# Reading a sub-layer's norm factors from PSUM, adding the last tile's squares inside the product with ones, and keeping the last two row tiles in SBUF

## The chip, the cores and the metric

One core of one Trainium2 chip runs the whole program. The metric is device time in microseconds from the start to the end of one execution. TensorE (PE) multiplies matrices and writes to PSUM; PEld is its weight load. VectorE (DVE), ScalarE (ACT) and GpSimd (POOL) work on elements. SyncE (SP) issues the transfers. Each engine has its own instruction stream and runs it in order.

## The reference, cut to what matters

Two layers. Each has two sub-layers (a mixer and a channel mixer), and the result of each is normalized over the 1024 features, scaled by a gain, and added to the residual `x`. The next sub-layer then normalizes `x` again.

```python
def _rmsnorm(x, w):
    xf = x.astype(jnp.float32)
    y = xf * lax.rsqrt(jnp.mean(xf * xf, axis=-1, keepdims=True) + NORM_EPS)
    return (y * w.astype(jnp.float32)).astype(x.dtype)

for l in range(DEPTH):                     # 2 layers, 512 tokens, 1024 features
    h = _rmsnorm(x, pre_mix_norm[l])
    h = _hybrid_mixer(h, ...)              # ends in  mixed @ w_out
    x = x + _rmsnorm(h, post_mix_norm[l])
    h = _rmsnorm(x, pre_ffn_norm[l])
    h = _conv_glu_ffn(h, ...)              # ends in  (gelu(gate) * val) @ ffn_down
    x = x + _rmsnorm(h, post_ffn_norm[l])
```

## The kernel before, in words

Activations are kept transposed: features on the 128 partitions, the 512 tokens along the free dimension. The residual `x` is eight row tiles of 128x512 (`xs(m)`). Every large product is done with operands split into a high and a low fp32r part, as three matmuls (`mmk`, line 310). Weights stream in as units; ACT rounds one to its high part and DVE or POOL subtracts to get the low part (`wlo`).

The order of instructions on each engine is fixed when the program is built, by a planner (`_Sched`, line 44). Jobs are Python generators; each operation has an estimated cost, each engine an estimated free time, and a job goes on when its planned time has come. Buffers are slots: `get` waits until a slot is planned to be free, `put` gives it back. The chip then runs each engine's stream in that order, held by semaphores.

`out_rows` (line 447) ends a sub-layer and runs four times: mixer and channel mixer of layer 0, then of layer 1. It computes eight result tiles `m` of 128 features.

- The first `full` tiles (five after a mixer, `nt` = 3; seven after a channel mixer, `nt` = 1) are computed for all 512 tokens in one PSUM bank (tag `g`, four banks). `evac` squares the bank into `sq`, adds that to the sum of squares `acc`, and for `m` below 6 writes the bank times the gain to an SBUF tile (tags A, B, C, two each). Tile 6 of a channel mixer stays in its bank.
- The last `nt` tiles, the tail, are computed for tokens 0 to 255 first (half 0) and then for tokens 256 to 511 (half 1). `tail_sum` squares each into the single buffer `vh` and adds it to `acc`. A tail tile below 6 is scaled to SBUF by DVE (`tail_evac`); tiles 6 and 7 stay in their banks.
- For each half, `chain` waits for the tail's sums and calls `row_rstd` (line 356): PE multiplies each 128-token column block of `acc` by a column of ones, which gives sums by token in PSUM; DVE divides by 1024 and adds epsilon; POOL raises to the power -0.5 (tile `rtp`); PE broadcasts the factors to all partitions (tile `pso`, the one bank of tag `o`); ACT copies them to the SBUF tile `rs`.
- Then eight `row` jobs start, 1.1 us apart in the plan. Each multiplies its tile by `rs` (tiles 6 and 7 by gain and `rs`, from PSUM), adds the product to `x` on DVE or POOL, and either stores `x` (end of the program) or has `scale_split` round and split it into `hx`, the input of the next sub-layer.

The next sub-layer begins with `lead`: three output tiles held in three PSUM banks (tag `s`), first over half 0 of `hx`, then over half 1, in the order in which the plan has `hx` ready. Its own factors come from `pre_rstd` (line 624), which uses the same `row_rstd` on the sums of squares `acc2` of the new `x`. The tiles of tags `acc2` and `rs` are free during the tail. While `sc.chain` is set, the low part of a weight unit goes to DVE.

In the profile, tiles are named by tag: A, B, C are the scaled row tiles, `psg`, `pss` and `pso` the PSUM banks, `vh` the tail's squares. All matmuls have line 138, ACT's operations line 147, DVE's and POOL's tensor_tensor line 151, the scalar_tensor_tensor line 165.

Of the kernel before, what the change touches and what calls it, by code (L numbers as in the profile page):

```python
# [10 lines left out]
F32 = mybir.dt.float32  # L11
F32R = mybir.dt.float32r
AF = mybir.ActivationFunctionType
ALU = mybir.AluOpType
# [4 lines left out]
P = 128  # L19
S = 512  # L20
D = 1024
KD = D // P
# [7 lines left out]
EPS = 1e-6  # L30
# [83 lines left out]
def kernel(ctx: ExitStack, tc: tile.TileContext, xT, w_ab, w_cm, w_tm, w_o, w_up, w_dn,  # L114
# [9 lines left out]
    kp = ctx.enter_context(tc.tile_pool(name="kp", bufs=1))  # L124
# [4 lines left out]
    sc = _Sched()  # L129


    def mm(ps, lhsT, rhs, start, stop):
        n = rhs.free_size()
        if rhs.dtype == F32R:
            sc.t += n / 2400.0 if n >= 256 else 0.107
        else:
            sc.t += max(0.214 if lhsT.free_size() > 64 else 0.11, n / 600.0)
        pe.matmul(ps, lhsT, rhs, start=start, stop=stop)  # L138
# [6 lines left out]
    def act(out_, in_, func, after=0.0, **kw):  # L145
        ptr = sum(1 for k in ("scale", "bias") if k in kw and not isinstance(kw[k], float))
        nc.scalar.activation(out_, in_, func, **kw)  # L147
        return sc.op("act", 0.1 + out_.free_size() * 8.3e-4 + 0.09 * ptr, after)

    def tt(out_, a, b, op, after=0.0, eng="dve"):  # L150
        (nc.vector if eng == "dve" else nc.gpsimd).tensor_tensor(out_, a, b, op=op)  # L151
        n = out_.free_size()
        return sc.op(eng, 0.07 + n * 1.05e-3 if eng == "dve" else 0.18 + n * 2.07e-3, after)

    def ts(out_, a, s1, s2, op0, op1=None, after=0.0, eng="dve"):
        e = nc.vector if eng == "dve" else nc.gpsimd
        if op1 is None:
            e.tensor_scalar(out_, a, s1, None, op0=op0)  # L158
        else:
            e.tensor_scalar(out_, a, s1, s2, op0=op0, op1=op1)  # L160
        n = out_.free_size()
        return sc.op(eng, 0.07 + n * 1.0e-3 if eng == "dve" else 0.17 + n * 8.5e-4, after)

    def stt(out_, a, s, b, op0, op1, after=0.0):
        nc.vector.scalar_tensor_tensor(out_, a, s, b, op0=op0, op1=op1)  # L165
        return sc.op("dve", 0.07 + out_.free_size() * 1.05e-3, after)
# [14 lines left out]
    BUFS = {"A": 2, "B": 2, "C": 2, "sq": 2, "acc": 1, "acc2": 1, "vh": 1, "rs": 1}  # L181
    PB = {"g": 4, "s": 3, "o": 1}

    def work(tag, cols=512, dt=F32):
        return kp.tile([P, cols], dt, tag=tag, bufs=BUFS[tag], name=tag)
# [8 lines left out]
    def pget(tag):  # L194
        yield from sc.get("ps" + tag, PB[tag])
        return psum(tag)

    def pput(tag, at):
        sc.put("ps" + tag, at)
# [10 lines left out]
    one = cc[:, C_ONE:C_ONE + 1]  # L210
# [135 lines left out]
    vv = load_vec(0)  # L346
# [6 lines left out]
    rc = load_row(0)  # L353
    sc.set(("vec", 0))

    def row_rstd(acc, seg, dst, tok):

        t0, t1 = seg
        c0, c1 = t0 // P, t1 // P
        ps = yield from pget("o")  # L360
        for c in range(c0, c1):
            mm(ps[:, c:c + 1], acc[:, c * P:(c + 1) * P], one, True, True)
        r = ts(tok[:, c0:c1], ps[:, c0:c1], 1.0 / D, EPS, ALU.mult, ALU.add)
        yield r
        nc.gpsimd.tensor_tensor(tok[:, c0:c1], tok[:, c0:c1], mhalf[:, c0:c1], op=ALU.pow)  # L365
        r = sc.op("pool", 0.17 + 0.15 * (c1 - c0), r)
        yield r
        for c in range(c0, c1):
            mm(ps[:, c * P:(c + 1) * P], tok[:, c:c + 1].to_broadcast([P, P]), ident, True, True)
        r = act(dst[:, t0:t1], ps[:, t0:t1], AF.Copy)  # L370
        pput("o", r)
        return r
# [74 lines left out]
    def out_rows(key, nt, rhs, nk, post, pre, dst, wait_rhs=None, flags=None):  # L447
# [3 lines left out]
        acc = work("acc")  # L451
        hw, sums = {}, []

        full = 8 - nt

        def evac(m, ps):
            if m == 0:
                r = act(acc, ps, AF.Square)
            else:
                sq = yield from wget("sq")  # L460
                r = act(sq, ps, AF.Square)
            if m < 6:
                r2 = ts(hw[m], ps, vv[:, post + m:post + m + 1], None, ALU.mult)
                pput("g", max(r, r2))
            if m:
                yield r
                r = tt(acc, acc, sq, ALU.add, eng="dve" if m == full - 1 else "pool", after=r)
                sc.put("sq", r)
            sc.set((key, "sum", m), r)

        def done(m, ps):
            if m < 6:
                yield from sc.get("ABC"[m % 3], 2)
                hw[m] = work("ABC"[m % 3])
            else:
                hw[m] = ps
            sc.spawn(evac(m, ps), 0)

        m0 = 0
# [53 lines left out]
        for _ in range(nt * ((nk + 7) // 8)):  # L533
            u = yield from take()
            us.append(u)
        yield from sc.get("rs", 1)
        rs = work("rs")
        hx = acc2 = None
        if pre is not None:
            yield from sc.get("acc2", 1)  # L540
            acc2 = work("acc2")
            hx = new_hx()
        left = {"m": 16}

        def row(m, seg, tail, after):
            t0, t1 = seg
            x = xs(m)[:, t0:t1]
            r = rs[:, t0:t1]
            if m < 6:
                h = hw[m][:, t0:t1]  # L550
                d = tt(h, h, r, ALU.mult, after=after)
            else:
                h = (tail[m] if m in tail else hw[m])[:, t0:t1]
                d = stt(h, h, vv[:, post + m:post + m + 1], r, ALU.mult, ALU.mult, after=after)
            yield d
            pool = m in ((1, 3, 5) if pre is not None or not t0 else (0, 1, 3, 4))
            d = tt(x, x, h, ALU.add, after=d, eng="pool" if pool else "dve")
            if m >= 6 and (m in tail or t0):
                pput("g", d)
            if m < 6 and t0:  # L560
                sc.put("ABC"[m % 3], d)
            yield d
            if pre is None:
                sync.dma_start(dst[:, m, t0:t1], x)
            else:
                yield from scale_split(key, m, seg, hx, vv[:, pre + m:pre + m + 1], acc2, d)
            left["m"] -= 1
            left[t0] = left.get(t0, 8) - 1
            if not left[t0]:
                sc.set(("rows", key, t0))  # L570

        def tail_evac(m, ps, seg):
            t0, t1 = seg
# [4 lines left out]
        def tail_sum(m, ps, seg):  # L578
            t0, t1 = seg
            yield sc.t + 0.1  # L580
            sq = yield from wget("vh")
            r = act(sq[:, t0:t1], ps[:, t0:t1], AF.Square)
            yield r
            yield from sc.wait(*[(key, "sum", j) for j in range(full)])
            r = tt(acc[:, t0:t1], acc[:, t0:t1], sq[:, t0:t1], ALU.add, after=r)
            sc.put("vh", r)
            sc.set((key, "tail", m, t0), r)

        def chain(seg, tail):
            t0, t1 = seg  # L590
            yield from sc.wait(*[(key, "tail", m, t0) for m in tail])
            yield sc.t + 0.1
            r = yield from row_rstd(acc, seg, rs, kp.tile([P, 4], F32, tag="rtp", bufs=2, name="rtp"))
            yield r
            for m in range(KD):
                sc.spawn(row(m, seg, tail, r), 0, at=r + 1.1 * m)
            if t0:
                sc.put("acc", r)
                while left["m"]:
                    yield sc.t + 0.2  # L600
                sc.set((key, "out"))

        nu = (nk + 7) // 8
        for seg in HALVES:
            tail = {}
            for i, m in enumerate(range(full, 8)):
                ps = yield from pget("g")
                tail[m] = ps
                for kt in range(nk):
                    mmk(ps, us[i * nu + kt // 8], kt % 8, rhs(kt), seg, kt == 0, kt == nk - 1)  # L610
                    if seg[0] and (kt % 8 == 7 or kt == nk - 1):
                        free(unit=u0 + i * nu + kt // 8)
                    yield
                sc.spawn(tail_sum(m, ps, seg), 0)
                if m < 6:
                    if m not in hw:
                        yield from sc.get("ABC"[m % 3], 2)
                        hw[m] = work("ABC"[m % 3])
                    sc.spawn(tail_evac(m, ps, seg), 0)
            sc.spawn(chain(seg, tail), 0)  # L620
            sc.chain = True
        return hx, acc2, rs

    def pre_rstd(key, acc2, seg, rs, rt):
        yield from sc.wait(*[("sq", key, m, seg[0]) for m in range(KD)])
        r = yield from row_rstd(acc2, seg, rs, rt)
        sc.set(("rs", key, seg[0]), r)
        if seg[1] == S:
            sc.put("acc2", r)
# [931 lines left out]
```

## Time and profile before

| | |
|---|---|
| median of 3 runs | 1411.63 us (1410.67 to 1415.19) |
| profiled execution | 1419.57 us, span 1417.5 us |
| mean granted TensorE clock | 0.981 |
| busy: PE, PEld, DVE, ACT, POOL | 1375.4, 1145.6, 861.9, 618.0, 719.2 us |
| moved by DMA | 123.17 MB |

Times in the trace count from the start of the span. A share of busy time is a mean over stages with different limits, so the stretches around the four calls of `out_rows` are looked at by themselves. A wait is put down to the instruction that came last by the profile.

### The profile page before, as it was taken

To read this page: it belongs to the slowest core of one execution; us is meant where nothing else is said; L and a number is where in the kernel's file an instruction comes from. 1 tells how busy PE (TensorE), PEld (TensorE's weight loads), DVE (VectorE), ACT (ScalarE), POOL (GpSimd) and SP (SyncE) were. 2 spreads that over 40 slices of the span, in tenths; PEclk is the share of its full clock that TensorE was granted. 3 is DMA by queue.
4 is the path that set the end of the run, shared out by engine and by line. 5 is a ranking of instruction groups with operands and counts; after the bars stand their busy time and mean duration, and the time that the engine had idled before them with its cause. 6 is when DMAs were issued, how large, how long until landed. Compare 5 with 4: busy or idle time off the path is not lost. (4 is left out here: it accounts for less than half of the span.)

```text
span 1417.5 us, 19282 instructions
## 1 busy us (share of the span) xinstructions
PE 1375.4 (97%) x7174; PEld 1145.6 (81%) x7174; DVE 861.9 (61%) x1512; ACT 618.0 (44%) x998; POOL 719.2 (51%) x778
## 2 busy tenths in 40 slices
PE   9999999998999999999989999999989999999996
PEld 5878777887888888888878887788888888888886
DVE  4774477847677777421569544778478777773213
ACT  5553466635544344232345433665345444433220
POOL 5455266414577777334173541663155777772441
PEclk9999999999999999999999987999999999999998
DMA  5233111052233232333332330110512333333331
GB/s 200 75 94 87 61 46 45 16 164 75 72 92 104 90 105 89 94 98 99 98 131 68 116 88 16 45 46 23 171 60 79 100 97 98 94 96 88 106 93 60
DMA packets 48701, 123.17 MB, mean 87 GB/s; under 512 B 15584, under 2 KB 18400, under 8 KB 48608
## 3 DMA queue, kind: packets, MB, share of 16 engines
q1 hardware_dynamic: 48608, 121.95, 27.8%
q8 instruction: 57, 0.93, 0.3%
q14 instruction: 36, 0.29, 0.1%
HBM read 115.11 MB, written 6.82 MB: 86 GB/s over the span
## 5 line engine op out<-in xcount | busy, mean ns | idle before, releaser
L151 POOL TENSOR_TENSOR wlo<-raw,whi 128x256 fp32r<-128x256 f32 x560 | 500.8, 925 | 357.9 <-ACT whi L147 343.9
L138 PE MATMUL psg<-hx,whi 128*128 128x512 f32 (+1 forms) x2080 | 631.9, 387 | 2.4 <-DVE hx L151 2.4
L138 PEld LDWEIGHTS psg<-hx,whi 128*128 128x128 f32 x2080 | 379.9, 189 | 76.1 <-DVE hx L151 3.4
L138 PE MATMUL psg<-hx,wlo 128*128 128x512 f32 (+1 forms) x1040 | 396.5, 381 | 0.0
L147 ACT ACTIVATE whi<-raw 128x1024 fp32r<-128x1024 f32 (+1 forms) x200 | 209.0, 1045 | 428.1 <-PE psg L138 367.5
L138 PEld LDWEIGHTS psg<-hx,wlo 128*128 128x128 f32 x1040 | 196.3, 189 | 38.2
L165 DVE SCALAR_TENSOR_TENSOR B<-A,vv,B 128x510 f32<-128x510 f32 (+1 forms) x176 | 199.4, 1135 | 39.3 <-ACT B L147 36.1
L138 PE MATMUL psg<-hid,whi 128*128 128x512 f32 (+1 forms) x744 | 213.1, 371 | 0.0
L138 PEld LDWEIGHTS psg<-hid,whi 128*128 128x128 f32 x744 | 135.6, 188 | 24.1
L151 DVE TENSOR_TENSOR wlo<-raw,whi 128x1024 fp32r<-128x1024 f32 (+1 forms) x58 | 73.7, 1273 | 133.6 <-ACT whi L147 133.6
L138 PE MATMUL psg<-hid,wlo 128*128 128x512 f32 (+1 forms) x372 | 137.9, 371 | 0.0
L138 PE MATMUL psg<-whi,hx 128*128 128x512 f32 x384 | 125.0, 407 | 0.7 <-DVE A L151 0.7
L151 POOL TENSOR_TENSOR acc<-acc,sq 128x256 f32<-128x256 f32 (+1 forms) x65 | 65.8, 1013 | 104.4 <-ACT sq L147 102.5
L151 DVE TENSOR_TENSOR A<-psg,rs 128x512 f32<-128x512 f32 x100 | 68.7, 689 | 40.8 <-PE psg L138 38.8
L138 PEld LDWEIGHTS psg<-whi,hx 128*128 128x128 f32 x384 | 70.1, 191 | 14.6 <-DVE A L151 1.5
L138 PEld LDWEIGHTS psg<-hid,wlo 128*128 128x128 f32 x372 | 70.0, 188 | 12.0
L138 PE MATMUL psg<-wlo,hx 128*128 128x512 f32 x192 | 76.2, 397 | 0.0
L147 ACT ACTIVATE B<-A,vv 128x512 f32<-128x512 f32 x88 | 70.2, 802 | 2.6 <-DVE A L151 2.6
L147 ACT ACTIVATE C<-B 128x512 f32<-128x512 f32 x44 | 27.7, 630 | 86.2 <-DVE B L165 86.1
L151 DVE TENSOR_TENSOR hid<-C,hid 128x512 fp32r<-128x512 f32 x44 | 36.3, 826 | 28.3 <-ACT hid L147 28.3
L158 POOL TENSOR_SCALAR B<-B,den 128x512 f32<-128x512 f32 (+1 forms) x30 | 41.0, 1368 | 23.8 <-DVE den L177 13.7
L138 PE MATMUL pss<-hx,whome 128*128 128x256 f32 x288 | 42.6, 305 | 5.2 <-DVE hx L165 4.6
(239 smaller groups left out, 1704.8 us busy)
## 6 DMA issues: line engine op xcount, KB each, us to landing
raw<-in_w_up_dram SPq DMA_DIRECT2D x88, 512.0 KB, 3.5
raw<-in_w_cm_dram SPq DMA_DIRECT2D x32, 512.0 KB, 3.6
raw<-in_w_dn_dram SPq DMA_DIRECT2D x32, 512.0 KB, 3.5
raw<-in_w_tm_dram SPq DMA_DIRECT2D x24, 512.0 KB, 3.5
raw<-in_w_o_dram SPq DMA_DIRECT2D x16, 512.0 KB, 3.5
raw<-in_w_dn_dram SPq DMA_DIRECT2D x16, 384.0 KB, 3.1
xt<-in_xT_dram SPq DMA_DIRECT2D x7, 512.0 KB, 7.0
scr_a<-am SPq DMA_DIRECT2D x8, 256.0 KB, 2.7
```

Source lines behind the costliest of these rows:

```text
L138: pe.matmul(ps, lhsT, rhs, start=start, stop=stop)
L147: nc.scalar.activation(out_, in_, func, **kw)
L151: (nc.vector if eng == "dve" else nc.gpsimd).tensor_tensor(out_, a, b, op=op)
L158: e.tensor_scalar(out_, a, s1, None, op0=op0)
L165: nc.vector.scalar_tensor_tensor(out_, a, s, b, op0=op0, op1=op1)
```

## The change

`row_rstd` takes a list of sums and sums their products with ones in PSUM. Called by `chain`, it gets the tile `po` of tag `o`, which `out_rows` now takes once and holds for both halves until the last row is done. It leaves the factors there, and `row` multiplies by `po` instead of `rs`. The squares of tile 7 are no longer added to `acc` by DVE: they stay in `vh` and go into the product as a second summand. `vh` is given back when the broadcast has been issued.

Tiles 6 and 7 get SBUF tiles, of the tags `acc2` and `rs`. In `evac` every full tile is scaled to SBUF by DVE; in the tail, ACT writes tiles 6 and 7 times the gain, right behind their Square, and gives the bank back. All rows are then one multiply from SBUF by PSUM and one add. At the end of the program the rows of a half start 0.3 us apart in the plan, and in half 1 POOL adds tiles 0, 2, 4, 6 instead of 0, 1, 3, 4.

```diff
-    def row_rstd(acc, seg, dst, tok):
+    def row_rstd(sums, seg, dst, tok, ps=None):
         t0, t1 = seg
         c0, c1 = t0 // P, t1 // P
-        ps = yield from pget("o")
+        keep = ps is not None
+        if not keep:
+            ps = yield from pget("o")
+        sm = ps[:, t0:t0 + c1 - c0]
         for c in range(c0, c1):
-            mm(ps[:, c:c + 1], acc[:, c * P:(c + 1) * P], one, True, True)
-        r = ts(tok[:, c0:c1], ps[:, c0:c1], 1.0 / D, EPS, ALU.mult, ALU.add)
+            for i, a in enumerate(sums):
+                mm(sm[:, c - c0:c - c0 + 1], a[:, c * P:(c + 1) * P], one, i == 0, i == len(sums) - 1)
+        yield sc.t + 0.1
+        r = ts(tok[:, c0:c1], sm, 1.0 / D, EPS, ALU.mult, ALU.add)
...
             mm(ps[:, c * P:(c + 1) * P], tok[:, c:c + 1].to_broadcast([P, P]), ident, True, True)
+        if keep:
+            return sc.t + 0.1
         r = act(dst[:, t0:t1], ps[:, t0:t1], AF.Copy)
...
-            if m < 6:
-                r2 = ts(hw[m], ps, vv[:, post + m:post + m + 1], None, ALU.mult)
-                pput("g", max(r, r2))
+            r2 = ts(hw[m], ps, vv[:, post + m:post + m + 1], None, ALU.mult)
+            pput("g", max(r, r2))
...
+        def row_tile(m):
+            if m not in hw:
+                tag = "ABC"[m % 3] if m < 6 else ("acc2", "rs")[m - 6]
+                yield from sc.get(tag, BUFS[tag])
+                hw[m] = work(tag)
...
-        yield from sc.get("rs", 1)
-        rs = work("rs")
-        hx = acc2 = None
+        yield from row_tile(6)
+        yield from row_tile(7)
+        acc2, rs = hw[6], hw[7]
+        hx = None
         if pre is not None:
-            yield from sc.get("acc2", 1)
-            acc2 = work("acc2")
             hx = new_hx()
         left = {"m": 16}
+        po = yield from pget("o")
 
         def row(m, seg, tail, after):
             t0, t1 = seg
             x = xs(m)[:, t0:t1]
-            r = rs[:, t0:t1]
-            if m < 6:
-                h = hw[m][:, t0:t1]
-                d = tt(h, h, r, ALU.mult, after=after)
-            else:
-                h = (tail[m] if m in tail else hw[m])[:, t0:t1]
-                d = stt(h, h, vv[:, post + m:post + m + 1], r, ALU.mult, ALU.mult, after=after)
+            r = po[:, t0:t1]
+            h = hw[m][:, t0:t1]
+            d = tt(h, h, r, ALU.mult, after=after)
             yield d
-            pool = m in ((1, 3, 5) if pre is not None or not t0 else (0, 1, 3, 4))
+            pool = m in ((1, 3, 5) if pre is not None or not t0 else (0, 2, 4, 6))
             d = tt(x, x, h, ALU.add, after=d, eng="pool" if pool else "dve")
-            if m >= 6 and (m in tail or t0):
-                pput("g", d)
...
+            if not left["m"]:
+                pput("o", d)
...
             r = act(sq[:, t0:t1], ps[:, t0:t1], AF.Square)
+            if m >= 6:
+                pput("g", act(hw[m][:, t0:t1], ps[:, t0:t1], AF.Copy, scale=vv[:, post + m:post + m + 1]))
+            if m == KD - 1:
+                last[t0] = sq
+                sc.set((key, "tail", m, t0), r)
+                return
             yield r
             yield from sc.wait(*[(key, "sum", j) for j in range(full)])
             r = tt(acc[:, t0:t1], acc[:, t0:t1], sq[:, t0:t1], ALU.add, after=r)
...
             yield from sc.wait(*[(key, "tail", m, t0) for m in tail])
+            yield from sc.wait(*[(key, "sum", j) for j in range(full)])
             yield sc.t + 0.1
-            r = yield from row_rstd(acc, seg, rs, kp.tile([P, 4], F32, tag="rtp", bufs=2, name="rtp"))
+            r = yield from row_rstd([acc, last[t0]], seg, None, kp.tile([P, 4], F32, tag="rtp", bufs=2, name="rtp"),
+                                    po)
+            sc.put("vh", sc.t)
             yield r
+            step = 1.1 if pre is not None else 0.3
             for m in range(KD):
-                sc.spawn(row(m, seg, tail, r), 0, at=r + 1.1 * m)
+                sc.spawn(row(m, seg, tail, r), 0, at=r + step * m)
```

More of the change, by code (lines that the diff above doesn't have):

```diff
@@ L469, in evac @@
             sc.set((key, "sum", m), r)
-        def done(m, ps):
-            if m < 6:
-                yield from sc.get("ABC"[m % 3], 2)
-                hw[m] = work("ABC"[m % 3])
-            else:
-                hw[m] = ps
+        def row_tile(m):
[3 more added lines that the diff above has]
+                hw[m] = work(tag)
+        def done(m, ps):
+            yield from row_tile(m)
             sc.spawn(evac(m, ps), 0)
@@ L547, in row @@
             x = xs(m)[:, t0:t1]
-            r = rs[:, t0:t1]
-            if m < 6:
-                h = hw[m][:, t0:t1]
-                d = tt(h, h, r, ALU.mult, after=after)
-            else:
-                h = (tail[m] if m in tail else hw[m])[:, t0:t1]
-                d = stt(h, h, vv[:, post + m:post + m + 1], r, ALU.mult, ALU.mult, after=after)
+            r = po[:, t0:t1]
+            h = hw[m][:, t0:t1]
+            d = tt(h, h, r, ALU.mult, after=after)
             yield d
-            pool = m in ((1, 3, 5) if pre is not None or not t0 else (0, 1, 3, 4))
+            pool = m in ((1, 3, 5) if pre is not None or not t0 else (0, 2, 4, 6))
             d = tt(x, x, h, ALU.add, after=d, eng="pool" if pool else "dve")
-            if m >= 6 and (m in tail or t0):
-                pput("g", d)
             if m < 6 and t0:
@@ L587, in tail_sum @@
             sc.set((key, "tail", m, t0), r)
+        last = {}
         def chain(seg, tail):
@@ L615, in out_rows @@
                 if m < 6:
-                    if m not in hw:
-                        yield from sc.get("ABC"[m % 3], 2)
-                        hw[m] = work("ABC"[m % 3])
+                    yield from row_tile(m)
                     sc.spawn(tail_evac(m, ps, seg), 0)
@@ L625, in pre_rstd @@
         yield from sc.wait(*[("sq", key, m, seg[0]) for m in range(KD)])
-        r = yield from row_rstd(acc2, seg, rs, rt)
+        r = yield from row_rstd([acc2], seg, rs, rt)
         sc.set(("rs", key, seg[0]), r)
```

## The prediction

> **What bounds the kernel now.** I read the page first, then busy time by stretch, then what TensorE (PE) waited for at each boundary, then the chain at the end.
>
> ```profile
> span 1417.5 us, 19282 instructions
> 320.00:350.00 30.00, 25.03 (x179) 23.18 (x177) 26.70 (x52) 16.80 (x37) 14.80 (x17) 0.94 0.26 85
> 350.00:680.00 330.00, 330.00 (x1475) 273.94 (x1475) 186.75 (x197) 128.24 (x165) 194.83 (x208) 1.00 0.31 94
> 680.00:735.00 55.00, 51.06 (x382) 47.04 (x382) 32.54 (x63) 21.80 (x45) 24.35 (x26) 1.00 0.32 107
> 735.00:1020.00 285.00, 278.29 (x1557) 228.58 (x1557) 184.47 (x447) 141.38 (x257) 123.26 (x136) 0.95 0.23 72
> 1020.00:1066.00 46.00, 41.42 (x287) 38.84 (x286) 31.69 (x61) 21.37 (x46) 19.73 (x24) 0.93 0.23 71
> 1390.00:1418.00 28.00, 15.02 (x124) 14.54 (x122) 12.40 (x29) 1.54 (x4) 6.98 (x9) 0.83 0.23 76
> ```
>
> After each stretch's length come PE, weight loads, VectorE (DVE), ScalarE (ACT), GpSimd (POOL), the granted clock and DMA. In the channel mixer (350 to 680) PE is busy for all 330.00 us: nothing there can be gained by another engine. The changed function runs four times, at the ends of sub-layers. I call these boundaries 1 to 4 (the stretches from 320, 680, 1020 and 1390). PE idles 5.0, 3.9 and 4.6 us in the first three and 13.0 us in the last. DVE is busy 26.7 of 30 us at boundary 1.
>
> What PE waited for around boundaries 1, 2 and 3 (total, times, longest):
>
> ```profile
> PE pso L138 <- DVE acc L151: 2.3, 2, 2.0
> PE pss L138 <- DVE hx L165: 2.0, 4, 0.8
> PE pso L138 <- POOL rtp L365: 0.7, 1, 0.7
> ...
> PE pss L138 <- DVE hx L165: 2.7, 5, 0.8
> ...
> PE pss L138 <- DVE hx L165: 2.6, 2, 2.1
> PE pso L138 <- POOL rtp L365: 1.6, 2, 0.9
> ```
>
> The waits are for the sums (acc), the power (rtp) and the split of the next sub-layer's input (hx), so for the row work that this change touches. The end of the program is a bare chain (start, length):
>
> ```profile
> 1397.44 0.34 PE pso L138 x4
> ...
> 1403.80 0.39 ACT vh L147
> ...
> 1404.22 0.44 DVE acc L151
> ...
> 1404.70 0.62 PE pso L138 x4
> ...
> 1405.58 0.83 POOL rtp L365
> ...
> 1406.45 0.72 PE pso L138 x4
> ...
> 1407.20 0.39 ACT rs L147
> ...
> 1407.62 0.43 DVE A L151
> ...
> 1410.67 0.34 DVE A L151
> ...
> 1414.36 0.42 DVE xt L151
> ```
>
> Square, add, product with ones, power, broadcast, copy, then rows: the last add ends at 1414.78 and the last store follows it by 2.7 us.
>
> **The change, part by part.** Durations first, from the trace by tile (least, median, most, in ns) and the grouped lines (busy us, mean ns):
>
> ```profile
> L151 DVE TENSOR_TENSOR A<-psg,rs x100: 671/692/695, 54.9 to 1282.3; 128x512 f32<-128x512 f32 x100
> L151 DVE TENSOR_TENSOR xt<-xt,psg x16: 405/409/422, 335.9 to 1414.4; 128x256 f32<-128x256 f32 x16
> L151 DVE TENSOR_TENSOR xt<-xt,C 128x256 f32<-128x256 f32 x9 | 6.1, 678 | 0.1
> L151 DVE TENSOR_TENSOR C<-C,rs 128x256 f32<-128x256 f32 x16 | 8.6, 538 | 0.0
> L151 DVE TENSOR_TENSOR B<-B,rs 128x256 f32<-128x256 f32 x16 | 7.8, 486 | 0.0
> L151 DVE TENSOR_TENSOR A<-A,rs 128x256 f32<-128x256 f32 x16 | 7.2, 452 | 4.2 <-ACT rs L147 4.2
> L165 DVE SCALAR_TENSOR_TENSOR psg<-psg,vv,rs 128x256 f32<-128x256 f32 x16 | 7.7, 482 | 0.0
> ```
>
> *Factors stay in PSUM.* One ACT copy (1407.20 to 1407.62, 0.42 us) leaves the chain of each half. The row multiplies now read one operand from PSUM. The rows show what that does: 100 multiplies with a PSUM operand spread over 24 ns while POOL was busy half the time, and the 16 adds that read psg over 17 ns; the same add with both operands in SBUF averages 678 ns. So the multiplies of tiles 0 to 5 fall from 452, 486 and 538 ns to about 411: 0.041 + 0.075 + 0.127 = 0.243, by four of each per boundary, 0.97 us. I take it whole as DVE time.
>
> *Tiles 6 and 7 move to SBUF.* Four multiplies per boundary go from 482 to 411 ns: 0.28 us less. Their four adds lose the PSUM operand: between 0 and 4 x (0.678 - 0.409) = 1.08 us more; I take 0.78, near the upper end, because POOL's work has to overlap something. ACT gets twelve scaled copies of tail tiles for eight factor copies, so four more of 0.39 us in all; its 16.8 of 30 us at boundary 1 cover that, and the copy stands behind the Square on its queue, so the chain does not see it. Uncovered, it would be 0.4 us per boundary. After the channel mixer, tile 6 also costs a full-width DVE scale, while DVE waits for sums: nothing. PSUM banks come free earlier, but no PE wait in the lists is for a bank: nothing.
>
> *The last tile's squares go into the product.* One DVE add per half (1404.22 to 1404.70, 0.48 us) leaves the chain. PE issues four more matmul records per half, 0.34 us by the first row of the chain. Where the squares are late, the first column's sum can be issued ahead, so I charge the exposed chain 0.2. The single vh buffer is now held until half 0's broadcast, so the next half's first Square is later; DVE idles in that stretch, so nothing, else one add's 0.4 us.
>
> *One PSUM tile for both halves.* This adds a wait. The trace shows how two engines share a bank:
>
> ```profile
> DVE A L158 <- ACT acc L147: 27.3, 4, 11.3
> ```
>
> That scale reads a psg bank and waits for the Square that only reads the same bank. If PE and DVE are ordered like that on the new tile, half 1's product must wait for every half 0 multiply placed ahead of it, and the next sub-layer's matmuls queue behind it on PE; multiplies placed behind wait for PE. Before, the products and the fifth and last half 0 multiplies stood so:
>
> ```profile
> 328.66 0.61 PE L138 MATMUL pso<-cc,acc 128*128 128x1 f32 x4 [2.03 <-DVE acc L151]
> 329.99 0.41 DVE L151 TENSOR_TENSOR B<-B,rs 128x256 f32<-128x256 f32 x1
> 334.40 0.48 DVE L165 SCALAR_TENSOR_TENSOR psg<-psg,vv,rs 128x256 f32<-128x256 f32 x1
> 701.37 0.50 PE L138 MATMUL pso<-cc,acc 128*128 128x1 f32 x4
> 701.84 0.41 DVE L151 TENSOR_TENSOR B<-B,rs 128x256 f32<-128x256 f32 x1
> 705.31 0.48 DVE L165 SCALAR_TENSOR_TENSOR psg<-psg,vv,rs 128x256 f32<-128x256 f32 x1
> 1035.36 0.50 PE L138 MATMUL pso<-cc,acc 128*128 128x1 f32 x4
> 1035.73 0.41 DVE L151 TENSOR_TENSOR B<-B,rs 128x256 f32<-128x256 f32 x1
> 1039.67 0.48 DVE L165 SCALAR_TENSOR_TENSOR psg<-psg,vv,rs 128x256 f32<-128x256 f32 x1
> ```
>
> Rows still start 1.1 us apart in the plan at boundaries 1 to 3, so I expect four or five multiplies ahead. Waiting for the fifth would hold the product by 1.74, 0.88 and 0.78 us (330.40 - 328.66 and so on), 3.4 in sum. I take nothing: PE waits for hx afterwards anyway (2.0, 2.7 and 2.6 us), and those waits shrink instead. At boundary 4 the step is 0.3, half 0's rows are done before the product, and nothing waits. The tile is also held until the last row, and the next sub-layer's factors need it; they are computed after the last split already.
>
> The Trainium skill, "PSUM — Partial Sum Buffer", section on bank collisions, speaks here against the change: two engines must not be in one bank at the same time, whatever the columns. The 27.3 us row agrees, for ACT and DVE; by that rule the 3.4 us would be a certain hold of the product and not a possible one.
>
> *Sum for boundaries 1 to 3.* DVE work in the bound stretch falls by 0.97 + 0.28 + 0.48 - 0.78, about 0.95. At boundary 1 DVE limits to the end: -1.0. At boundary 2 two products' 0.34 lie on a busier PE, half of it felt after the waits: -0.5. At boundary 3 what counts is the broadcast of half 1, after which PE runs through: 0.42 + 0.48 less the exposed 0.2, and 0.1 for DVE's lighter load ahead of it: -0.8. Together -2.3; bounds -5.3 (the 7.3 that PE waits for hx there less six extra products of 0.34) and +3.4.
>
> *Boundary 4.* Chain: +0.34 (half 0's products push the last matmul), -0.48 (add), +0.2, -0.42 (copy): -0.36. Then the rows: from 1407.62 to 1414.78 DVE runs 15 instructions in 7.16 us (0.477 each), three of them leftovers of half 0, which now run earlier. Twelve remain: 12 x 0.477 = 5.7 at the old mean, 12 x 0.34 = 4.1 at the undisturbed pitch (the chain's multiply at 1410.67); I take 5.1, as eight are now multiplies with a PSUM operand. That is -2.06; with the chain -2.4, bounds -1.8 and -3.4. POOL still adds four of these rows, others than before, and SyncE's sixteen stores follow the adds in their new order: nothing.
>
> Total: -2.3 - 2.4 = -4.7. The profiled execution took 1419.57 us, 2.07 more than its span, and lies 7.9 us above the median 1411.63; a difference between traces carries over: 1411.63 - 4.7 = **1406.9 us**. Replanning the second mixer (285 us with 6.7 us of PE idle) may add or take 1.5.
>
> **The rivals.**
> - *Only the end gains.* The adds of tiles 6 and 7 collide as often as the multiplies did, and PE's extra products eat the rest. For: adds with two SBUF operands reach 678 ns. Against: boundary 1 is 89% DVE. 1411.63 - 2.4 = 1409.2. The five-multiply hold uncovered gives 1410.3, also no change.
> - *The collisions vanish.* Multiplies immune and nothing shifted to the adds: per boundary 0.97 + 0.28 + 0.48 = 1.73, and 4.1 us at the end: -5.2 - 3.4 = -8.6, 1403.0. For: the 24 ns spread; against: the adds stay exposed. The Trainium skill, "SBUF — State Buffer", section "Who interferes with whom", states it as a rule: a DVE instruction with at most one SBUF input does not contend with GpSimd, one with two does. The rows agree (671 to 695 against 678 for half the elements).
> - *Slower: the bank order.* If all eight half 0 multiplies stand ahead of half 1's product, PE stands until 334.88, 705.79 and 1040.15: 6.2 + 4.4 + 4.8 = 15.4, less the later waits of 2.0 + 2.7 + 2.6: +8.1. With -2.4 that is 1417.3. It decides from the seventh multiply on. Against: the 1.1 us step in the plan.
> - *The end is limited by the stores.* Stores close up as rows do; with 1 us of the gain lost, 1407.9.
>
> **How the numbers follow.** About 0.3% (4.2 us) is what a measurement can tell from no change. Likeliest case 0.40, own range 1404.5 to 1409, two thirds of it beyond 1407.4; collisions vanish 0.15; only the end (with the hold) 0.27; stores 0.06; bank order 0.12. Faster: 0.27 + 0.15 + 0.03; slower 0.12; the rest the same. The range from 1402.5 to 1412.5 leaves out the slower case and a little below.
>
> **What would show it.** No ACT rs copy from rtp factors and no acc add ahead of the last products; multiplies by pso near 411 ns with a narrow spread; adds of tiles 6 and 7 spread like the others; rows of half 0 finished before half 1's product at the end, and the last add 2 to 2.5 us earlier. PE's hx waits at boundaries 1 to 3 shorter. A PE product waiting for a DVE multiply for over 2 us, or DVE multiplies waiting for PE, would make me wrong on the slow side.

## The result, and the profile after

The change made the kernel slower: median 1424.96 us (1423.92 to 1429.44) against 1411.15 us (1408.32 to 1415.19) in the same comparison, ratio 1.0101 [1.0077, 1.0124]. 1406.9 was predicted. The profiled execution took 1423.92 us, span 1422.1.

The table cuts the span at the starts of the same matmuls in every kernel: boundaries 1 and 3 from the first output-projection product to the last lead matmul; boundary 2 from the last product of layer 0's channel mixer with a `wlo` operand (the products with `wxu` follow for 2.2 us) to the last lead matmul; the second mixer from there to its output projection; the end from the last `wlo` product of layer 1's channel mixer to the end of the span. Single profiles, in us; "before" is a second profile of the unchanged kernel (the first experiment).

| | boundary 1 | boundary 2 | second mixer | boundary 3 | end |
|---|---|---|---|---|---|
| before | 73.69 | 29.03 | 250.47 | 75.48 | 16.74 |
| after | 75.36 | 28.55 | 261.82 | 76.04 | 13.23 |
| difference | +1.67 | -0.48 | +11.35 | +0.56 | -3.51 |

The stretch ahead of boundary 1, in which no kernel here changes the work, takes 277.6 to 281.5 us in their profiles, so a difference of one or two microseconds in a single profile is not yet a finding. A length alone can mislead by more: in the first profile of the kernel before, the second mixer took 259.2 us, with the granted clock at half for 24 us in one piece. PE's idle time tells the two apart: it was 7.9 us in that profile, too. The same stretches by engine, in windows (PE, weight loads, DVE, ACT, POOL, granted clock, DMA): before,

```profile
724.60:975.10 250.50, 242.44 (x1414) 197.82 (x1413) 168.62 (x435) 130.78 (x244) 125.20 (x139) 0.99 0.23 70
1394.30:1411.10 16.80, 4.29 (x29) 3.70 (x27) 10.80 (x25) 0.77 (x2) 6.28 (x8) 0.64 0.37 125
```

and after:

```profile
727.30:989.10 261.80, 246.53 (x1413) 199.28 (x1412) 168.16 (x437) 133.44 (x248) 106.15 (x119) 0.97 0.22 68
752.30:777.30 25.00, 19.70 (x95) 15.43 (x94) 22.55 (x37) 17.36 (x25) 6.94 (x8) 0.87 0.18 64
1408.90:1422.10 13.20, 4.10 (x33) 3.74 (x31) 7.74 (x21) 0.75 (x2) 5.37 (x7) 0.76 0.48 159
```

PE has the same number of matmuls in the mixer (one record fewer), but idles 15.3 us instead of 8.1, and needs 4.1 us more for them at a lower granted clock; a third of the idle time is in one slice of 25 us. No line of the mixer was changed.

What PE waited for around boundaries 1, 2 and 3 after (total, times, longest):

```profile
PE pss L138 <- DVE hx L165: 2.7, 1, 2.7
PE pso L138 <- DVE rs L151: 1.5, 1, 1.5
...
PE pso L138 <- DVE B L151: 1.9, 1, 1.9
PE pss L138 <- DVE hx L165: 0.2, 1, 0.2
...
PE pso L138 <- DVE rs L151: 2.4, 1, 2.4
PE pss L138 <- DVE hx L165: 2.3, 1, 2.3
```

New is the wait of a product (`pso`) for a DVE row multiply: `rs` is tile 7, the last of half 0's eight, `B` the fifth. In order of time at boundary 1:

```profile
334.05 0.41 DVE L151 TENSOR_TENSOR rs<-rs,pso 128x256 f32<-128x256 f32 x1
334.51 0.58 PE L138 MATMUL pso<-cc,acc 128*128 128x1 f32 x2 [1.55 <-DVE rs L151]
336.24 5.04 PE L138 MATMUL pss<-hx,whome 128*128 128x256 f32 x24
341.12 0.60 PE L138 MATMUL pso<-cc,rtp 128*128 128x128 f32 x4
341.76 0.42 DVE L151 TENSOR_TENSOR A<-A,pso 128x256 f32<-128x256 f32 x1 [3.39 <-PE pso L138]
```

Half 1's product is held for the eighth multiply. Its broadcast then stands behind 24 lead matmuls, and DVE, the busiest element engine at this boundary before (26.7 of 30 us), waits 3.39 us for it. The row multiplies and their adds, by form:

```profile
L151 DVE TENSOR_TENSOR A<-A,pso 128x256 f32<-128x256 f32 x16 | 6.6, 414 | 13.6 <-PE pso L138 13.6
L151 DVE TENSOR_TENSOR B<-B,pso 128x256 f32<-128x256 f32 x16 | 6.6, 410 | 0.0
L151 DVE TENSOR_TENSOR C<-C,pso 128x256 f32<-128x256 f32 x16 | 6.5, 409 | 1.1 <-PE pso L138 1.1
L151 DVE TENSOR_TENSOR xt<-xt,acc 128x256 f32<-128x256 f32 x7 | 4.5, 643 | 0.0
L151 DVE TENSOR_TENSOR xt<-xt,rs 128x256 f32<-128x256 f32 x8 | 3.3, 414 | 0.0
```

and the chain at the end, where the add and the copy are gone:

```profile
1411.45 0.39 ACT vh L147
...
1411.88 0.84 PE pso L138 x6
...
1412.99 0.72 POOL rtp L371
...
1413.75 0.72 PE pso L138 x4
...
1414.50 0.42 DVE A L151
...
1418.09 0.53 DVE xt L151
```

This chain ends with the last add but one, at 1418.62. The last add of the half, that of tile 7 (`rs`), starts at 1418.54 and ends at 1418.95. From the first row multiply to the end of the last add it is 4.46 us (before: 7.16), and the span ends 3.2 us behind the last add (before: 2.7).

### The profile page after: what moved, and what is told of

Same layout as the page of the kernel before. It is cut to its first block, busy times and chain, and to the rows that moved or that the text cites. A ratio compares the mean times of both kernels' runs of the same rounds, so it can differ in the third digit from the quotient of the medians.

```text
span 1422.1 us, 19316 instructions
## 1 busy us (share of the span) xinstructions
PE 1376.0 (97%) x7206; PEld 1147.0 (81%) x7206; DVE 852.0 (60%) x1510; ACT 623.3 (44%) x1006; POOL 694.7 (49%) x758
## 5 line engine op out<-in xcount | busy, mean ns | idle before, releaser
L151 POOL TENSOR_TENSOR wlo<-raw,whi 128x256 fp32r<-128x256 f32 x544 | 484.1, 921 | 376.9 <-ACT whi L147 355.5
L151 DVE TENSOR_TENSOR wlo<-raw,whi 128x1024 fp32r<-128x1024 f32 (+1 forms) x62 | 77.8, 1258 | 152.0 <-ACT whi L147 152.0
L138 PEld LDWEIGHTS psg<-whi,hx 128*128 128x128 f32 x384 | 70.7, 193 | 16.3 <-DVE A L151 2.0
L158 POOL TENSOR_SCALAR B<-B,den 128x256 f32<-128x256 f32 (+1 forms) x28 | 36.9, 1319 | 25.7 <-DVE den L177 18.8
```

## The experiments

Theory A: the second mixer, whose order the planner works out anew when anything ahead of it moves, came out in a worse order, and the boundaries by themselves are worth little either way. Rival B: the shared PSUM bank holds PE and DVE at the boundaries, and that is the loss. All ratios are to the kernel before on the same chip; 0.1% is 1.4 us.

**1. The kernel before, unchanged**

> The kernel before, unchanged, for a second profile of it: the first one's execution (1419.57 us) lay 8 us above the median, with the granted clock at half for 24 us in the second mixer. If the second mixer is what the change made slow, this profile has it about 8 us shorter than the first, near 1411 us in all; ratio 1.000 +- 0.002. If the first profile was typical, 1419 again.

1413.08 us, ratio 1.0007 [0.9997, 1.0018]: this is how far the same kernel lies from itself. The profile has the second mixer 8.7 us shorter than the first profile (250.5 against 259.2 us), as expected.

**2. The new code at boundary 4 alone**

In experiments 2 to 4 and 8 to 10 the old functions stay, and the new ones are called at the boundaries named; the input's factors are computed by the old `row_rstd`.

```diff
-hx, acc2, rs = yield from out_rows((l, "f"), ...)
+hx, acc2, rs = yield from (out_rows_new if l == 1 else out_rows)((l, "f"), ...)
```

> The change at the last of the four boundaries alone; all code and order before it as in the kernel before. By the traces of before and after, the stretch from the last full-width matmul to the end shrank by 2.6 us: ratio 0.998, about 1408.6 us, when nothing else moves. If what costs the 13.8 us is in the changed instructions at every boundary, a quarter of it (3 us slower).

1409.48 us, 0.9984 [0.9970, 0.9998]. End 13.25 us by the trace, 3.5 shorter than in the profile of experiment 1 and 3.0 shorter than in the first profile of the kernel before (16.22). The difference between those two is the last broadcast, 1.22 us in one and 0.72 in the other, as it is after the change; so 3.0 is the fair figure. Ahead of this stretch, half 0's product takes eight matmuls instead of four, and the channel mixer of layer 1 is 0.45 us longer (344.22 against 343.77); 2.5 us are left. The runs give 2.9. This part is a gain.

**3. The new code at boundaries 3 and 4**

```diff
+... (out_rows_new if l == 1 else out_rows)((l, "m"), ...)
+... (out_rows_new if l == 1 else out_rows)((l, "f"), ...)
```

> The change at boundaries 3 and 4 alone (both calls of layer 1). The second mixer keeps its old instruction order, since nothing planned before it changes. Theory A, the second mixer was replanned and that is most of the loss: boundary 3 costs 1.7 us as in the trace of after, the end gives 2.6: 1410.3 us, ratio 0.999. Theory B, the loss lies in the changed boundaries themselves, about half of it here: 1418 us, ratio 1.005. Under both a PE product of half 1 waits for the eighth multiply of half 0 at boundary 3.

1412.72 us, 1.0012 [0.9993, 1.0031]. By the runs, boundary 3 gives back what the end gained (3.2 us more than in experiment 2); it takes 75.97 us, against 73.72 in experiment 2. With the mixer ahead of it in its old order, nothing like 14 us is lost: B alone doesn't explain the result.

**4. As 3, with a second bank for half 1**

```diff
-            if not left["m"]:
-                pput("o", d)
+            if not left[t0]:
+                pput("g" if t0 else "o", d)
...
+            pb = (yield from pget("g")) if t0 else po
...
-            r = yield from row_rstd_new([acc, last[t0]], seg, None, kp.tile(...), po)
+            r = yield from row_rstd_new([acc, last[t0]], seg, None, kp.tile(...), pb)
...
-            r = po[:, t0:t1]
+            r = pb[:, t0:t1]
```

> As the run for layer 1 alone, but half 1's sums and factors go to a bank of tag g of their own, so that no product of half 1 waits for a multiply of half 0. If the shared bank is what costs at boundary 3, the 1.7 us lost there turn into the gain that was forecast for it, 0.8: about 1407.8 us, 2.5 us less than the run with one bank. If the shared bank costs nothing, the same time as that run.

1410.19 us, 0.9981 [0.9960, 1.0001], 2.5 us less than experiment 3, as expected of the bank; but the trace doesn't put it there. PE's wait for a DVE multiply is gone, while boundary 3 takes 78.55 us in this profile (granted clock 0.89) and the mixer is short (247.4 us). The same boundary with two banks takes 73.85 and 74.08 us in experiments 9 and 12, so the 78.55 is not the price of the second bank. Inconclusive by itself.

**5 to 8. The order of the second mixer by itself**

Experiments 5 and 6 add one assignment to the planner's clock: 0.1 us in the kernel before, 0.2 us in the changed one. No work is added; what can differ is the order that the planner writes and which engine it gives a weight split to, and both do (below). Theory M in the expectations is A, and R says that the loss comes from the changed instructions themselves.

```diff
+            if l:
+                sc.t += 0.1
             mixt = yield from mixer(l, key, hx, acc2, rs, FULL if l == 0 else HALVES)
```

> The kernel before, every instruction the same, but the planner's clock is moved on by 0.1 us when the second mixer is planned, so that the order around and in that mixer comes out otherwise. Theory M: the loss of the changed kernel is a second order of the second mixer (261.8 instead of 250.5 us there) that a tenth of a microsecond in the plan is enough to bring about. Then this kernel takes 1420 to 1424 us without any part of the change, and its second mixer 259 to 262 us. Rival R: the loss comes from the changed instructions themselves (the tile held for both halves, tiles 6 and 7 in the buffers acc2 and rs that the mixer takes over late). Then it stays at 1411 to 1414.

1426.37 us, 1.0089 [1.0056, 1.0121]: the whole loss, without any part of the change, and somewhat more than was expected.

> The changed kernel, every instruction the same, with the planner's clock moved on by 0.2 us at the same place. M: the second mixer falls back to 248 to 251 us; what is left are the boundaries (+1.7 at the first, +0.5 at the third) and the end (-3): about 1411.6 us, 1409 to 1414. R: 1423 to 1426, as before the shift.

1411.73 us, 0.9996 [0.9972, 1.0020]: the whole loss gone, with every part of the change. Experiment 7 looks for the trigger:

```diff
-        yield sc.t + 0.1
+        if keep:
+            yield sc.t + 0.1
         r = ts(tok[:, c0:c1], sm, 1.0 / D, EPS, ALU.mult, ALU.add)
```

> The changed kernel, but the pause of 0.1 us that the change adds to the factors' job between product and division is made only for a result's factors, not for those of the next sub-layer's input. No instruction differs. M: this pause, which stands in the part of the change that was costed at nothing, is what turned the second mixer's order; without it 1409 to 1414 us (1411.6 by the boundaries' traces). R: 1423 to 1426. If M holds for the two shifted kernels and not here, the pause is not the trigger.

1414.74 us, 1.0006 [0.9987, 1.0025]. Boundaries 75.94, 31.24 and 75.99 us, end 13.24, mixer 249.0. Experiment 8:

```diff
+... (out_rows_new if l == 0 else out_rows)((l, "m"), ...)
+... (out_rows_new if l == 0 else out_rows)((l, "f"), ...)
```

> The new code at boundaries 1 and 2 alone, the input's factors by the old code (no added pause). M: the second mixer keeps its length (248 to 251 us), boundary 1 costs 1.7 and boundary 2 nothing: 1414 us, 1412 to 1415.5. R, with the loss in what layer 0 hands to the second mixer: 1421 to 1425.

1413.18 us, 0.9999 [0.9974, 1.0025], mixer 251.72 us: what layer 0 hands over does not make the mixer long. Boundary 2 takes 31.21 us, where no cost was expected. The mixers in windows, experiment 5, then 6, then 7:

```profile
726.90:990.00 263.10, 247.65 (x1414) 201.10 (x1413) 165.37 (x437) 133.97 (x248) 109.56 (x123) 0.97 0.23 69
```

```profile
732.20:978.80 246.60, 239.33 (x1414) 195.41 (x1413) 168.46 (x434) 130.35 (x243) 127.94 (x142) 1.00 0.23 70
```

```profile
731.20:980.30 249.10, 240.84 (x1414) 196.47 (x1413) 168.50 (x435) 130.74 (x244) 125.44 (x139) 0.99 0.23 70
```

The first half of A is shown: old code with the other plan is long (263.1 us), new code with a plan like the old one is short. PE's idle time in the mixer separates the two kinds in all profiles: 15.3 to 16.3 us in the changed kernel and in experiments 5, 11 and 12, and 7.3 to 8.9 us in the other ten. What differs can be read from two tiles (duration least/median/most, then first and last start). The scan's products by `edec` and the attention's by `pt`, before,

```profile
L138 PE MATMUL pss<-C,edec x32: 275/275/377, 939.1 to 960.0; 128*128 128x128 f32 x32
L138 PE MATMUL pso<-pt,vh x32: 220/278/388, 872.8 to 969.1; 128*128 128x256 f32 x16, 128*128 128x128 f32 x16
```

and in experiment 5:

```profile
L138 PE MATMUL pss<-C,edec x32: 271/275/377, 959.9 to 980.9; 128*128 128x128 f32 x32
L138 PE MATMUL pso<-pt,vh x32: 221/279/574, 880.2 to 957.1; 128*128 128x256 f32 x16, 128*128 128x128 f32 x16
```

Counted from the mixer's start (724.6 and 726.9), the scan's products come 18.5 us later and the attention's last one by `pt` 14.3 us earlier. In the short order the last product by `pt` stands 9.1 us behind the scan's last, in the long one 23.8 us ahead of it: the two strands are interleaved otherwise. These two tiles stand the long way in the changed kernel and in experiments 11 and 12, too. The plans differ in a second thing: in the mixer DVE makes the low part of 8 or 9 weight units in the long ones and of 4 in before and in experiment 7, and GpSimd does less (123 instructions against 139 above). Which of the two makes PE idle more no run separates; that it is the interleaving is argued, not shown, and which of the planner's choices tips first stays open.

**9. The changed kernel without that pause, with two banks at all boundaries**

The new code is called at all four boundaries, with the second bank of experiment 4; the input's factors are computed by the old `row_rstd`, which has no pause. As in 4, the bank of half 0 is given back after that half's eighth row, so the input's factors of half 0 can be computed earlier (their first product comes 67.9 us into boundary 1, in experiment 7 73.0); what that is worth by itself no run separates from the second bank.

> The changed kernel without the added pause in the input's factors, and at all four boundaries half 1's sums and factors get a PSUM bank of their own (tag g) instead of the second half of the held tile. Bank theory: at boundaries 1 and 2 PE's product no longer waits for a DVE multiply (2.3 and 1.9 us in the kernel with one tile), and each boundary gets about 2 us shorter than there (75.95 and 31.24 us from the first product of the tail's sub-layer to the last of the lead): about 1410 us, 1408 to 1412. Rival, queue order: DVE waits for the broadcast of half 1, which stands behind the lead's matmuls on PE in either case, and the boundaries stay as long: 1412 to 1415.

1404.67 us, 0.9934 [0.9921, 0.9947]: the fastest version here, faster than both kernels, and faster than the 1408 to 1412 us that the bank theory expected. Against 7, boundary 1 is 3.19 us shorter (72.75), boundary 2 4.53 (26.71) and boundary 3 2.14 (73.85): 9.9 together. At boundary 2, experiment 7 in order of time, and three windows of it,

```profile
703.87 0.42 DVE L151 TENSOR_TENSOR B<-B,pso 128x256 f32<-128x256 f32 x1
704.34 0.57 PE L138 MATMUL pso<-cc,acc 128*128 128x1 f32 x2 [1.92 <-DVE B L151]
706.23 0.42 DVE L151 TENSOR_TENSOR C<-C,pso 128x256 f32<-128x256 f32 x1 [1.94 <-PE pso L138]
707.26 0.63 PE L138 MATMUL pss<-hx,whi 128*128 128x256 f32 x2
```

```profile
700.00:731.20 31.20, 29.22 (x216) 27.62 (x215) 23.23 (x46) 16.73 (x37) 17.43 (x20) 0.89 0.20 51
704.30:707.70 3.40, 3.36 (x16) 3.22 (x17) 1.47 (x4) 0.51 (x1) 1.21 (x3) 0.51 0.27 112
708.60:712.00 3.40, 3.40 (x22) 3.26 (x21) 1.91 (x6) 2.26 (x6) 0.00 (x0) 0.62 0.00 0
```

and experiment 9, the same two views:

```profile
696.42 0.28 PE L138 MATMUL psg<-cc,acc 128*128 128x1 f32 x2
698.36 0.41 DVE L151 TENSOR_TENSOR C<-C,pso 128x256 f32<-128x256 f32 x1
698.47 0.40 PE L138 MATMUL pss<-hx,whi 128*128 128x256 f32 x2
```

```profile
694.10:720.90 26.80, 26.04 (x217) 24.96 (x216) 22.51 (x47) 16.71 (x37) 17.93 (x20) 1.00 0.23 63
```

With one tile the product waits 1.92 us for the fifth multiply, the next multiply waits 1.94 us for PE, and from the hold's end the granted clock is at half for 6.8 us (704.4 to 711.2; the third window takes in its last 2.6 us): a pair of lead matmuls takes 0.63 us instead of 0.40, and PE is busy 3.2 us longer with the same work. So the shared bank costs, as edited here; the rival that said the broadcast's place on PE decides is not settled: DVE still waits 2.2 us for it at boundary 1.

**10. Boundary 4 alone, with the old order of its rows**

```diff
-            step = 1.1 if pre is not None else 0.3
+            step = 1.1
...
-            pool = m in ((1, 3, 5) if pre is not None or not t0 else (0, 2, 4, 6))
+            pool = m in ((1, 3, 5) if pre is not None or not t0 else (0, 1, 3, 4))
```

> The new code at boundary 4 alone, with the old order of its rows (1.1 us apart in the plan, GpSimd adds tiles 0, 1, 3, 4 of half 1). If the 3.3 us that the stretch from the last power to the end gets shorter come mainly from rows of half 0 that run earlier and from the new spread of the adds, it gives back 1 to 2 of them: 1410.5 to 1412. If they come from the multiplies reading PSUM and the copy that is gone, it keeps them: 1409 to 1410.

1411.84 us, 0.9997 [0.9975, 1.0020]; the end takes 14.76 us. The interval holds both answers; the trace says that, of the 3.0 us (16.22 to 13.24), 1.5 come from the order of the rows and 1.5 from the multiplies and the shorter chain.

**11. The kernel before, with a larger shift**

The edit of 5 with 0.8 in place of 0.1.

> The kernel before with the planner's clock moved on by 0.8 us instead of 0.1 ahead of the second mixer. The plan comes out in a third order; by the planner's own clock its second mixer is half as much longer than the undisturbed one as that of the 0.1 us shift. If the planner's clock ranks the orders, 1416 to 1420 us; if any disturbed order costs the same, 1422 to 1428; if orders are good or bad by things that the plan doesn't know, anything else, 1410 included.

1422.96 us, 1.0067 [1.0054, 1.0079], mixer 260.61 us. The planner's own clock had put this order half way, and the chip puts it with the bad one: here what the planner thought of an order was no forecast.

**12. The changed kernel, pause kept, two banks**

> The changed kernel as it is, with the added pause, and with a second bank for half 1 at all four boundaries. If the order of the second mixer and the shared bank are two separate losses, the mixer stays at 260 to 263 us and the boundaries fall as in the kernel with two banks and no pause: 1404.7 + 11 to 12 = 1415 to 1418 us. If the second bank alone is what made that kernel fast (the mixer too), 1404 to 1408. If the long mixer came from the boundaries' late ends, it shortens in part: 1408 to 1414.

1418.44 us, 1.0044 [1.0030, 1.0058]: boundaries as in 9 (72.91, 26.74, 74.08), mixer 264.64 us. The two losses are separate and add up. The long mixer does not need the shared bank, and a boundary does not need the short mixer to gain. By differences of the ratios, the order of the mixer is 0.95% (after against 7) or 1.10% (12 against 9), 13 to 16 us; the shared bank 0.57% (after against 12) or 0.72% (7 against 9), 8 to 10 us.

## Why the prediction was wrong

*The term that failed* is the last one of the sum: "Replanning the second mixer (285 us with 6.7 us of PE idle) may add or take 1.5". It took 11.4 us by the traces and 13 to 16 by the runs. I had read PE's idle time there as the amount at stake. That bounds what a better order can win; what a worse order can lose it doesn't bound at all. Every rival was placed at a boundary, so none had this mechanism, and no range built from them could hold it. What tipped the plan was a pause of 0.1 us, in a helper that the next sub-layer's factors also use: with it the mixer is long (after, 12), without it short (7, 9), and a shift of 0.2 us behind it undoes it (6). There is nothing bad in the pause itself: a shift of 0.1 us does the same to the old kernel. The part-by-part list counted instructions and so passed over a line that issues none.

*The bank's hold, "I take nothing"*, failed too. The order was as I expected at boundary 2 (five multiplies ahead) and not at 1 and 3 (all eight). My reason for nothing was that PE waits for `hx` afterwards and that those waits shrink. They did at boundary 2 (2.7 to 0.2), and yet between 7 and 9 the hold cost there most: the multiplies behind it wait for PE in turn, and the clock falls. That difference is 9.9 us at the three boundaries. The rival of the bank order, which I gave 0.12, put them at +8.1 where the likeliest case had -2.3, a difference of 10.4. That its size comes close is luck: it added up holds of 15.4 us and took off 7.3 of other waits, and the holds measured 5.8 us in sum; the waits in return and the clock make up for what is missing. Its condition (eight multiplies ahead) was met at boundaries 1 and 3; at boundary 2 five were enough for a loss. The Trainium skill's "PSUM — Partial Sum Buffer", section on bank collisions, which I had weighed and set aside, was the better guide: by it two engines are not to be in one bank at the same time, so each product behind a reader of its bank is a certain hold. Each of the three changed boundaries shows one (1.5, 1.9 and 2.4 us).

*The multiplies* were right: 411 ns forecast, 414, 410 and 409 measured. *The adds of tiles 6 and 7* were overpriced: 643 and 414 ns, so (0.234 x 7 + 0.005 x 8) / 4 = 0.42 us per boundary, where I took 0.78.

*Boundaries 1 to 3.* I had -1.0, -0.5 and -0.8. All profiles together, in us:

| | boundary 1 | boundary 2 | boundary 3 |
|---|---|---|---|
| old code | 73.7 to 75.4 (8 profiles) | 28.8 to 29.2 (8) | 72.5 to 75.5 (7) |
| new code, one tile | 75.4 to 76.2 (4) | 28.6 once, 31.2 (3) | 76.0 to 78.8 (4) |
| new code, two banks | 72.8, 72.9 | 26.7, 26.7 | 73.9, 74.1, 78.6 |

Against the mean of the old code, the two banks of experiment 9 give -1.6, -2.3 and +0.2. So with the hold away a gain is shown at boundaries 1 and 2, larger than forecast, and none at boundary 3, where the spread of the old code is wider than the forecast of -0.8. With one tile, experiment 7 has +1.6, +2.2 and +2.4.

*Boundary 4.* Forecast -2.4, bounds -1.8 and -3.4; measured -2.5 by the traces of experiment 2 and the first profile, and 1409.48 against 1412.37 by the runs. Half 0's products cost 0.45 (taken: 0.34). From the start of the end's stretch to the first row multiply the chain is 0.76 us shorter (0.23 up to the start of the last power, 4.31 to 4.08, and 0.53 behind it, with the copy's 0.42 in it), where the terms came to 0.70 (0.48 - 0.2 + 0.42). The row stretch is 4.46 us, between my lower bound of 4.1 and the 5.1 taken: POOL, which still adds four rows, hardly disturbs multiplies with a PSUM operand. The stores, put at nothing, take 0.5 back: the span ends 3.2 us behind the last add and not 2.7. So this sum comes out, in part because the last two errors nearly cancel.

Experiment 9 is the change with its two losses removed. Its 1404.67 us lie inside my own range around 1406.9, but that is partly luck: on its chip the kernel before took 1413.53, so the gain is about 9 us where I forecast 4.7. The rival in which the collisions vanish had 8.6, with 1.73 at each of the three boundaries. The stages above come to about 6 us, and where the rest is gained no run shows.

## What to carry to other kernels

Where a planner fixes the order when the program is built, as here, an edit can also be a draw of a new order for every stage behind it. Before pricing or judging an edit, shift the planner's clock by a tenth of a microsecond in the unchanged kernel and see what the time does; here that spread (14 us) was three times the gain that I forecast. Compare by stage, at the same instructions, and look first at stages that were not touched.

A PSUM tile that one engine still reads while another is to write its other half was one lock here, not two halves. Give the second half a bank of its own, or count the readers ahead of the writer and charge the hold, the wait in return, and the clock after it.

## What the runs showed of the hardware

A hold of 1.92 us on PE in experiment 7 was followed by 6.8 us at half of the clock (the windows above), and so it was at the same place in experiments 6 and 8. The Trainium skill, "TensorE: Matmul & The Clock Gate", Part 1, names a window of about 3.4 us and a halved rate, which agrees: the stretch is two such windows long. Its rule speaks of idle gaps longer than the window, and this one was shorter. The same hold of 1.9 us in the changed kernel's own profile at boundary 2 left the clock at 1.00:

```profile
698.80:727.30 28.50, 26.32 (x215) 24.83 (x215) 22.66 (x46) 16.59 (x37) 17.31 (x20) 1.00 0.24 62
```

So the same hold may or may not cost 3 us more: boundary 2 takes 28.55 us there against 31.24 in experiment 7. What decides it, no run here shows.
